# Queries' squared norms of eight heads: from transposes on the matrix engine to block transposes on the vector engine

## The chip, the cores and the metric

The kernel runs on one core of a Trainium2 chip. A core has a matrix engine (PE, with its weight loads shown apart as PEld), a vector engine (DVE), a scalar engine (ACT), a general engine (POOL) and a queue engine (SP) that issues transfers. Each engine works through its own list of instructions in order and waits on semaphores where it needs another's result. The metric is the device time of one execution in microseconds (us).

## The reference

One decoder layer for 1024 prompt tokens (16 learned tokens stand before them) and 8 sample tokens. All head inputs come from one combined projection; two groups of heads follow, four of an mLSTM and eight of a gated delta rule (GDN); a gate, an output projection and a final norm end it. What matters here, for a GDN head (`qg`, `kg` have 128 entries for each token and head):

```
qkv = silu(causal_conv(q|k|v))
qg  = l2norm(qg) * 128 ** -0.5        # x * rsqrt(sum(x * x) + EPS)
kg  = l2norm(kg)
S, og = chunked(gdn_chunk, S, (qg, kg, vg, beta, g))
yg  = head_rms(og) * w_gnorm * silu(z_g)   # h * rsqrt(mean(h * h) + EPS)
```

`og` is linear in `qg`, so a query's norm is only a factor of its output row, and the head norm that follows divides it out again but for its EPS. The kernel therefore leaves the queries unscaled and puts their squared norm into the EPS term of the head norm.

## The kernel before, in words

Everything is kept with features on the 128 partitions and tokens along the free axis. The activations are held as two parts of reduced precision (`xh`, `xl`) and so are the weights (`wh`, `wl`); a projection of one 128-column tile of the weights over all tokens is 3 blocks of tokens by 8 slices of the inner axis by 3 products, 72 matmuls of some 350 columns, written to `pjg` (GDN), `pjz` (gate z of the GDN heads), `pjm` (mLSTM), `pjo` and `pjzm` (gates of the mLSTM heads).

These projections are the filler of PE's list. The generator `filler` walks over the jobs in a fixed order: for each GDN head its k, v and q projections, and after head `h` as many z projections as `ZS[h]` says, then the mLSTM heads, the left z projections, and the gates. All other work (convolutions, the inverse of each head's triangular matrices, the merge, the chains) is written as generators ("threads"), and `Plan.run` records the instructions of all of them in the order in which its own clocks of the engines say that they can go on; when no thread can, the filler gives the next four matmuls. So one order per engine is fixed when the kernel is built. `Plan.note` holds the durations that the planner reckons with; for a vector instruction they go by the size of its output.

The change lies in `gdn_chain(h)`, one head's recurrence over a chunk of 16 tokens and eight chunks of 128. Its inner `prepare(c)` turns k and v of the chunk on PE (`tp<-ident,kq`, `tp<-ident,v`), in the kernel before q as well, and makes k.q (`sk<-kq`). ACT squares the turned q and sums along the row (`jq<-tp`, with an accumulator read after it) into `ss[:, 0, c-1]`. A step then goes: `sk<-S` and `tp<-S` on PE, `R` on DVE, `up<-R` on PE, `wv` on ACT, `up<-wv` on PE, the new state `S` and the output rows `oo` on DVE, whose squares go to `ss[:, 1]`. At the chain's end two small DVE instructions put the two sums into `hst[:, 4 + h]`, the buffers of keys, queries and values go back to their rings (`r_kq`, three buffers; `r_v`, four), and `("C", h)` is marked done. `head_norms` waits for all eight and makes the reciprocal roots `rsg` in one go; `gate(8 + h)` scales the output rows by them. Projections of head `h + 3` need the ring buffer that chain `h` gives back.

Of the kernel before, what the change touches and what calls it, by code (L numbers as in the profile page):

```python
# [12 lines left out]
F32 = mybir.dt.float32  # L13
F32R = mybir.dt.float32r
I32 = mybir.dt.int32
AF = mybir.ActivationFunctionType
ALU = mybir.AluOpType
# [3 lines left out]
P = 128  # L21
D = 1024
KT = D // P
META = 16
SEQ = 1024
NS = 8
TP = META + SEQ
NT = TP + NS
MH, GH = 4, 8
NCH = 1 + SEQ // P  # L30
EPS = 1e-6
BIG = 1e30
MDK = 128.0
# [239 lines left out]
RISE = (4, 6, 3)  # L273
MERGE = 0.5
SAMPLE = 1.5
ZS = (1, 2, 2, 0, 1, 1, 0, 1)


def weight_tiles():
# [12 lines left out]
def chunk(c):  # L292
    return (0, META) if c == 0 else (META + P * (c - 1), P)
# [3 lines left out]
def hymba_kernel(ctx: ExitStack, tc: tile.TileContext, a: dict, o: dict):  # L297
    nc = tc.nc
    plan = Plan()
    dve, act, pool, pe = (  # L300
        Engine(plan, n, e) for n, e in (("dve", nc.vector), ("act", nc.scalar), ("pool", nc.gpsimd), ("pe", nc.tensor)))
# [8 lines left out]
    def bank(tag, name):  # L310
        t = ps.tile([P, 512], F32, tag=tag, name=name, bufs=BANKS[tag])
        plan.take(tag, BANKS[tag], t)
        return t

    def room(tag):
        return plan.room(tag, BANKS[tag])

    def pst(name):
        return bank("s", name)

    def pst2(name):
        return bank("k", name)


    ident = cp.tile([P, P], F32, name="ident")
# [98 lines left out]
    gp = ctx.enter_context(tc.tile_pool(name="gp", bufs=1))  # L424
# [17 lines left out]
    wk = ctx.enter_context(tc.tile_pool(name="wk", bufs=2))  # L442
# [6 lines left out]
    hst = gp.tile([P, GH + MH, 8], F32, name="hst")  # L449
# [7 lines left out]
    def w(tag, shape, name, bufs=2):  # L457
        t, names = wk.tile([P] + shape, F32, tag=tag, name=name, bufs=bufs), wnames.setdefault(tag, [""] * bufs)
        plan.follow(t, names[-bufs])
        names.append(t.tensor.name)  # L460
        return t
# [9 lines left out]
    done = set()  # L471

    def has(*key):
        return lambda: key in done
# [5 lines left out]
        xs.append((r, *r.get([D], f"xt{i}")))  # L480

    warm = w("xss", [2], "warm", NCH + 1)
    nrow = wk.tile([1, D], F32, tag="tmp", name="nrow", bufs=1)
    wgr = wp.tile([P, KT, P], F32, tag="wr", name="wrg")
    wgh_ = wk.tile([P, KT, P], F32R, tag="B", name="whg", bufs=1)
    wrs.append(wgr.tensor.name)
# [139 lines left out]
    def settings():  # L626

        pool.memset(phalf, 0.5)
        yield has("xc", 8)
        dve.tensor_scalar(wgh, wgn, 0.5, None, op0=ALU.mult)  # L630
        dve.tensor_scalar(wmq, wmn, 0.25, None, op0=ALU.mult)
        yield lambda: all(("xc", i) in done for i in range(NCH))
        for e in (ebuf[0], ebuf[1], db, wa, wb):
            pool.memset(e, 0.0)
            yield "pool"
        for e in vas:
            pool.memset(e[:, 256:257], 1.0)

    gr = wk.tile([P, NT], F32, tag="E", name="gr", bufs=1)
    gi, gbig = r_kq.get([2 * TP], "gb")  # L640
# [248 lines left out]
    hd = {}  # L889
# [148 lines left out]
    def gdn_chain(h):  # L1038

        yield lambda: ("M", h) in done and ("P", h, 0) in done  # L1040
        q_ = hd[h]
        (kq, v, ki, vi), gm, kap, em0, eb = hd[h, "P"], q_["gm"], q_["kap"], q_["em0"], ebuf[h % 2]
        pre = {}
        ss = w("ss", [2, 8], f"ss{h}")

        def prepare(c):
            c0, T = chunk(c)
            kc, qc = kq[:, 0, c0 : c0 + T], kq[:, 1, c0 : c0 + T]
            tp, sk, pm = pst(f"tp{h}_{c}"), None, None
            pe.transpose(tp[0:T, 0:P], kc, ident)  # L1050
            pe.transpose(tp[0:T, P : 2 * P], v[:, c0 : c0 + T], ident)
            if c > 0:
                pe.transpose(tp[:, 2 * P : 3 * P], qc, ident)
                sk = pst(f"sk{h}_{c}")
                pe.matmul(sk[:, 0:P], kc, qc, start=True, stop=True)
            kt = w("kt", [P], f"kt{h}_{c}")
            vt = w("vt", [P], f"vt{h}_{c}")
            act.activation(vt[0:T], tp[0:T, P : 2 * P], AF.Copy, scale=kap[0:T, 3, c : c + 1])
            act.activation(kt[0:T], tp[0:T, 0:P], AF.Copy, scale=kap[0:T, 2, c : c + 1])
            if c > 0:  # L1060
                jq = w("jm", [256], f"jq{h}_{c}", bufs=1)[:, 0:P]
                act.activation(jq, tp[:, 2 * P : 3 * P], AF.Square, accum_out=ss[:, 0, c - 1 : c])
                pm = w("pm", [P], f"pm{h}_{c}")
                dve.scalar_tensor_tensor(
                    out=pm, in0=sk[:, 0:P], scalar=kap[:, 1, c : c + 1], in1=gm[:, c, :], op0=ALU.mult, op1=ALU.mult)
            pre[c] = kt, vt, pm, tp, sk

        prepare(0)
        S = None
        yield pre[0][1]  # L1070
        for c in range(NCH):
            c0, T = chunk(c)
            kc, qc = kq[:, 0, c0 : c0 + T], kq[:, 1, c0 : c0 + T]
            kt, vt, pm, tp, sk = pre.pop(c)
            E2 = em0[0:T, 0:T] if c == 0 else eb[:, c - 1, :]
            R = vt
            if c > 0:
                pe.matmul(sk[:, P : 2 * P], kc, S, start=True, stop=True)
                pe.matmul(tp[:, 3 * P : 4 * P], qc, S, start=True, stop=True)
                R = w("R", [P], f"R{h}_{c}")  # L1080
                dve.scalar_tensor_tensor(
                    out=R, in0=sk[:, P : 2 * P], scalar=negc[:, c, h : h + 1], in1=vt, op0=ALU.mult, op1=ALU.add)
                qs = w("qs", [P], f"qs{h}_{c}")
                act.activation(qs, tp[:, 3 * P : 4 * P], AF.Copy, scale=egc[:, c, h : h + 1])
                yield R
            up = pst(f"up{h}_{c}")
            wq = up[:, 2 * P : 3 * P]
            pe.matmul(wq[0:T], E2, R[0:T], start=True, stop=True)
            wv = w("wv", [P], f"wv{h}_{c}")
            act.copy(wv[0:T], wq[0:T])  # L1090
            if c + 1 < NCH:
                prepare(c + 1)
            yield wv
            pe.matmul(up[:, 0:P], kt[0:T], wv[0:T], start=True, stop=True)
            if c > 0:
                pe.matmul(up[:, P : 2 * P], pm, wv, start=True, stop=True)
            Sn = w("S", [P], f"S{h}_{c}", bufs=3)
            if c == 0:
                dve.tensor_copy(Sn, up[:, 0:P])
            else:  # L1100
                dve.scalar_tensor_tensor(
                    out=Sn, in0=S, scalar=egend[:, c, h : h + 1], in1=up[:, 0:P], op0=ALU.mult, op1=ALU.add)
                oo = w("oo", [258], f"oo{h}_{c}", 3)[:, 0:P]
                dve.tensor_tensor(out=oo, in0=qs, in1=up[:, P : 2 * P], op=ALU.add)
                jq = w("jm", [256], f"jo{h}_{c}", bufs=1)[:, 0:P]
                act.activation(jq, oo, AF.Square, accum_out=ss[:, 1, c - 1 : c])
                sp.dma_start(h_d[8 + h, :, c - 1, :], oo)
            S = Sn
            yield S
        yield ss  # L1110
        dve.tensor_scalar(ss[:, 0], ss[:, 0], EPS * MDK, 4 * EPS * EPS * MDK, op0=ALU.mult, op1=ALU.add)
        dve.scalar_tensor_tensor(
            out=hst[:, 4 + h, :], in0=ss[:, 1], scalar=1.0 / P, in1=ss[:, 0], op0=ALU.mult, op1=ALU.add)
        sp.dma_start(o["p_S"][h], S)
        r_gm.free(q_["gi"])
        r_kq.free(ki)
        r_v.free(vi)
        done.add(("C", h))

    def rsqrt_wide(y, x, t):  # L1120

        dve.tensor_scalar(y.bitcast(I32), x.bitcast(I32), -0.5, float(0x5F3759DF), op0=ALU.mult, op1=ALU.add)
        for _ in range(3):
            dve.tensor_tensor(out=t, in0=y, in1=y, op=ALU.mult)
            dve.tensor_tensor(out=t, in0=t, in1=x, op=ALU.mult)
            dve.tensor_scalar(t, t, -0.5, 1.5, op0=ALU.mult, op1=ALU.add)
            dve.tensor_tensor(out=y, in0=y, in1=t, op=ALU.mult)
# [455 lines left out]
    def head_norms():  # L1583

        for heads in ([("C", h) for h in range(GH)], *([("mC", h)] for h in range(MH))):
            yield lambda: all(k in done for k in heads)
            h0 = heads[0][1] if len(heads) == 1 else MH
            n = slice(h0, h0 + len(heads))
            yield hst
            rsqrt_wide(rsg[:, n], hst[:, n], rst[:, 0 : len(heads)])  # L1590
            for i in range(len(heads)):
                done.add(("rs", h0 + i))
# [298 lines left out]
    def filler():  # L1891
        gdn, z = [list(gdn_jobs(h)) for h in range(GH)], [z_job(h) for h in range(GH)]
        jobs = [gate_job]
        for h, n in enumerate(ZS):
            jobs += gdn[h]
# [61 lines left out]
    def chains():  # L1957
        for h in range(GH):
            yield from gdn_chain(h)
        for h in range(MH):  # L1960
            yield from mlstm_chain(h)
# [94 lines left out]
```

## Time and profile before

| | before |
|---|---|
| three runs, median | 1205.81 us (1203.74 to 1205.92) |
| profiled execution, its own time | 1202.72 us |
| its span, from the first to the last instruction | 1200.9 us |
| PE busy | 1184.0 us, 99% |
| DVE, ACT, POOL busy | 852.2, 602.4, 487.9 us |

The 1.8 us between own time and span lie outside the first and last instruction. A busy share is an average: PE's ends are modelled, and matmuls overlap, so the distance from one start to the next says more than the length of one. The chains of the GDN heads fill about 167 to 614 us of the span.

### The profile page before, as it was taken

What the parts mean: (1) busy time and instruction counts of PE and PEld (TensorE: products, weight loads), DVE (VectorE), ACT (ScalarE), POOL (GpSimd) and SP (SyncE); (2) the same over time, 40 slices, a digit from 0 to 9 for tenths busy, and PEclk for the clock granted to TensorE, in tenths of its full rate; (3) what the DMA queues carried; (4) which work ended last, traced back from release to release, by engine and by line L of the source; (5) the groups of instructions that cost most, each with busy time, mean ns of one, the idle gap of its engine ahead of it and who ended that gap; (6) DMA issues with size and microseconds to landing.
All of it is one profiled execution on the core that took longest, in us unless ns stands there. A gap on an engine that the chain in (4) does not pass through costs nothing.

```text
span 1200.9 us, 23024 instructions
## 1 busy us (share of the span) xinstructions
PE 1184.0 (99%) x8314; PEld 1105.9 (92%) x8314; DVE 852.2 (71%) x2069; ACT 602.4 (50%) x1894; POOL 487.9 (41%) x648
## 2 busy tenths in 40 slices
PE   9999999999999999999999999999999999999997
PEld 7999999999999999999999999999999999876885
DVE  6789787587968588864356665546767665887986
ACT  7544455667565666554544453336543433333544
POOL 3105977827685756864012404230011111441432
PEclk9999999999999999999999999999999999999999
DMA  6032212212221221122122443535778878574352
GB/s 242 19 97 86 81 47 83 87 43 72 69 75 43 89 73 55 36 75 61 43 84 70 154 126 119 174 123 172 273 273 286 305 269 297 204 270 132 107 159 87
DMA packets 87084, 154.86 MB, mean 129 GB/s; under 512 B 26793, under 2 KB 48513, under 8 KB 86970
## 3 DMA queue, kind: packets, MB, share of 16 engines
q1 hardware_dynamic: 86776, 153.23, 38.1%
q8 instruction: 65, 1.06, 0.4%
q14 instruction: 49, 0.40, 0.1%
q10 hardware_dynamic: 194, 0.17, 0.0%
HBM read 107.65 MB, written 45.71 MB: 128 GB/s over the span
## 4 chain that ended last, share of the span: by engine, by line
PE 82%; DVE 9%; issue 5%; ACT 1%; POOL 1%; DMA 1%; POOLq 0%; SPq 0%; DVEq 0%; ACTq 0%
PE pjg L56 20%; PE pjm L56 13%; PE pjo L56 7%; PE pjz L56 7%; PE op L56 7%; PE pjzm L56 7%; PE up L56 4%; PE tp L56 3%; PE sk L56 2%; PE mnm L56 2%; DVE left L56 1%; PE mup L56 1%; PE hT L56 1%; DVE owl L56 1%; PE kk L56 1%
## 5 line engine op out<-in xcount | busy, mean ns | idle before, releaser
L56 PE MATMUL pjg<-xht,whg 128*128 128x350 f32 (+6 forms) x624 | 197.6, 324 | 1.0 <-ACT xht L56 1.0
L56 PE MATMUL pjg<-xlt,whg 128*128 128x350 f32 (+6 forms) x624 | 197.1, 323 | 0.0
L56 PE MATMUL pjg<-xht,wlg 128*128 128x350 f32 (+6 forms) x592 | 191.1, 326 | 0.0
L56 POOL TENSOR_TENSOR tmp<-B,E 33x31 f32<-33x31 f32 (+15 forms) x248 | 147.0, 593 | 75.3 <-DMA B<-nd 56.5
L56 POOL TENSOR_TENSOR E<-E,tmp 33x31 f32<-33x31 f32 (+15 forms) x248 | 156.0, 629 | 19.4
L56 PE MATMUL op<-owh,left 128*128 128x512 f32 x448 | 142.0, 396 | 2.1 <-DVE xr L56 1.8
L56 PE MATMUL pjm<-xht,wlm 128*128 128x350 f32 (+2 forms) x384 | 126.4, 329 | 0.0
L56 PE MATMUL pjm<-xht,whm 128*128 128x350 f32 (+2 forms) x384 | 126.4, 329 | 0.0
L56 PE MATMUL pjm<-xlt,whm 128*128 128x350 f32 (+2 forms) x384 | 126.2, 329 | 0.0
L56 PEld LDWEIGHTS pjg<-xht,whg 128*128 128x128 f32 x624 | 116.5, 189 | 1.8 <-issue 1.2
L56 PEld LDWEIGHTS pjg<-xlt,whg 128*128 128x128 f32 x624 | 116.5, 189 | 0.5
L56 PEld LDWEIGHTS pjg<-xht,wlg 128*128 128x128 f32 x592 | 111.0, 189 | 0.4
L56 PEld LDWEIGHTS op<-owh,left 128*128 128x128 f32 x448 | 84.0, 188 | 24.7 <-DVE xr L56 2.6
L56 DVE SCALAR_TENSOR_TENSOR kq<-cr,prm,kq 128x346 f32<-128x346 f32 (+7 forms) x147 | 92.1, 630 | 11.6 <-ACT cr L56 8.3
L56 PE MATMUL op<-owl,left 128*128 128x512 f32 x224 | 88.3, 394 | 0.0
L56 PEld LDWEIGHTS pjm<-xht,wlm 128*128 128x128 f32 x384 | 72.5, 189 | 0.8 <-issue 0.4
L56 PEld LDWEIGHTS pjm<-xlt,whm 128*128 128x128 f32 x384 | 72.4, 188 | 0.6 <-issue 0.4
L56 PEld LDWEIGHTS pjm<-xht,whm 128*128 128x128 f32 x384 | 72.4, 189 | 0.2
L56 POOL TENSOR_TENSOR ebuf<-ebuf,wb 128x1024 f32<-128x1024 f32 x8 | 15.7, 1965 | 122.7 <-DMA ebuf<-mvb_d 122.7
L56 PE MATMUL pjo<-xht,who 128*128 128x344 f32 x192 | 62.3, 324 | 0.6 <-DVE mg L56 0.6
L56 PE MATMUL pjz<-xlt,whz 128*128 128x344 f32 x192 | 62.8, 327 | 0.0
L56 PE MATMUL pjz<-xht,wlz 128*128 128x344 f32 x192 | 62.4, 325 | 0.0
(353 smaller groups left out, 3180.7 us busy)
## 6 DMA issues: line engine op xcount, KB each, us to landing
wrg<-in_wt SPq DMA_DIRECT2D x23, 512.0 KB
left<-c_d SPq DMA_DIRECT2D x40, 256.0 KB
wrm<-in_wt SPq DMA_DIRECT2D x16, 512.0 KB
ht<-h_d SPq DMA_DIRECT2D x16, 512.0 KB
gm<-rows_d SPq DMA_DIRECT2D x8, 576.0 KB
xt<-in_x_p SPq DMA_DIRECT2D x8, 512.0 KB
wrz<-in_wt SPq DMA_DIRECT2D x8, 512.0 KB
h_d<-oo SPq DMA_DIRECT2D x64, 64.0 KB
```

What stands on the lines that cost most here:

```text
L56: r = f(*args, **kw)
```

## The change

The transposes of q leave `prepare`, and with them the square and the accumulator read on ACT. A new thread `query_squares(h)`, started with the chain, takes the head's 1024 tokens of q in four pieces of 256: ACT squares a piece as it lies (features on partitions), DVE turns it in square blocks of 32 by 32, and DVE sums each block row, so that 8 sums for each partition are left (`squares[:, h, 8 * i : 8 * i + 8]`). A partition then holds, for 32 tokens, the sum over only 32 of the 128 features; the other three quarters stand on the other groups of 32 partitions. When all eight chains are done, `query_norms` adds the four groups for all heads in one product on PE with a 0/1 matrix `fold` (128 by 128, into 256 columns, `qsum`), and four DVE instructions add the result to `hst`. `fold` is built in `settings` by three small DVE and three small ACT instructions. The buffers of a head are given back only when its squares are made (`has("Q", h)`). One z projection moves from behind head 4 to behind head 3 (`ZS`). `nrow`, a row used at the start, takes another buffer (`E`), which makes room for the new tiles.

```diff
-ZS = (1, 2, 2, 0, 1, 1, 0, 1)
+ZS = (1, 2, 2, 1, 0, 1, 0, 1)
...
-    nrow = wk.tile([1, D], F32, tag="tmp", name="nrow", bufs=1)
+    nrow = wk.tile([1, D], F32, tag="E", name="nrow", bufs=1)
...
+        f0 = fold[:, 0:32]
+        dve.tensor_tensor(out=f0, in0=ident[:, 0:32], in1=ident[:, 32:64], op=ALU.add)
+        for i in (2, 3):
+            dve.tensor_tensor(out=f0, in0=f0, in1=ident[:, 32 * i : 32 * i + 32], op=ALU.add)
+        for i in (1, 2, 3):
+            act.copy(fold[:, 32 * i : 32 * i + 32], f0)
...
         ss = w("ss", [2, 8], f"ss{h}")
+        plan.add(query_squares(h))
...
             if c > 0:
-                pe.transpose(tp[:, 2 * P : 3 * P], qc, ident)
                 sk = pst(f"sk{h}_{c}")
...
             if c > 0:
-                jq = w("jm", [256], f"jq{h}_{c}", bufs=1)[:, 0:P]
-                act.activation(jq, tp[:, 2 * P : 3 * P], AF.Square, accum_out=ss[:, 0, c - 1 : c])
                 pm = w("pm", [P], f"pm{h}_{c}")
...
-        dve.tensor_scalar(ss[:, 0], ss[:, 0], EPS * MDK, 4 * EPS * EPS * MDK, op0=ALU.mult, op1=ALU.add)
-        dve.scalar_tensor_tensor(
-            out=hst[:, 4 + h, :], in0=ss[:, 1], scalar=1.0 / P, in1=ss[:, 0], op0=ALU.mult, op1=ALU.add)
+        dve.tensor_scalar(hst[:, 4 + h, :], ss[:, 1], 1.0 / P, 4 * EPS * EPS * MDK, op0=ALU.mult, op1=ALU.add)
         sp.dma_start(o["p_S"][h], S)
+        yield has("Q", h)
         r_gm.free(q_["gi"])
...
+    squares = gp.tile([P, GH, 32], F32, name="squares")
+    fold = gp.tile([P, P], F32, name="fold")
+
+    def query_squares(h):
+
+        q = hd[h, "P"][0][:, 1, META:TP]
+        for i in range(4):
+            yield "act"
+            sq, turned = w("sq", [256], f"sq{h}_{i}", bufs=1), w("sqt", [256], f"sqt{h}_{i}", bufs=1)
+            act.activation(sq, q[:, 256 * i : 256 * i + 256], AF.Square)
+            yield sq
+            yield "dve"
+            dve.transpose(turned, sq)
+            dve.tensor_reduce(squares[:, h, 8 * i : 8 * i + 8], turned.rearrange("p (b d) -> p b d", d=32), mybir.AxisListType.X, ALU.add)
+        done.add(("Q", h))
+
+    def query_norms():
+
+        yield squares
+        yield room("k")
+        pt = pst2("qsum")
+        pe.matmul(pt[:, 0 : 32 * GH], fold, squares.rearrange("p h b -> p (h b)"), start=True, stop=True)
+        yield pt
+        for r in range(4):
+            rows = slice(32 * r, 32 * r + 32)
+            part = pt[rows, 0 : 32 * GH].rearrange("p (h c r) -> p h c r", h=GH, r=4)[:, :, :, r]
+            dve.scalar_tensor_tensor(out=hst[rows, MH : MH + GH, :], in0=part, scalar=EPS * MDK, in1=hst[rows, MH : MH + GH, :], op0=ALU.mult, op1=ALU.add)
...
             yield lambda: all(k in done for k in heads)
+            if len(heads) > 1:
+                yield from query_norms()
```

PE's list has 6375 rows before and 6312 after: 64 fewer transposes, one product more. In head 7's chain (names carry head and chunk) the step from `R7_1` to `wv7_1` stood so on PE before:

```order
L56 MATMUL up7_1_8191<-R7_1_8183,ebuf1_102 128x128
L56 MATMUL tp7_2_8195<-ident_65,kq7_6587 128x128
L56 MATMUL tp7_2_8195<-ident_65,v7_6588 128x128
L56 MATMUL tp7_2_8195<-ident_65,kq7_6587 128x128
L56 MATMUL sk7_2_8199<-kq7_6587 128x128
```

and the same step in the changed kernel, with the four projection matmuls that stand behind it:

```order
L56 MATMUL up7_1_8230<-R7_1_8214,ebuf1_102 128x128
L56 MATMUL tp7_2_8234<-ident_65,kq7_6463 128x128
L56 MATMUL tp7_2_8234<-ident_65,v7_6464 128x128
L56 MATMUL sk7_2_8237<-kq7_6463 128x128
L56 MATMUL pjm0_3_2_8224<-xlt_77,whm0_3_7997 128x348
L56 MATMUL pjm0_3_2_8224<-xht_76,wlm0_3_7998 128x348
L56 MATMUL pjm0_3_2_8224<-xht_76,whm0_3_7997 128x348
L56 MATMUL pjm0_3_2_8224<-xlt_77,whm0_3_7997 128x348
L56 MATMUL up7_1_8230<-wv7_1_8232,kt7_1_8183 128x128
```

The second transpose from `kq7` (that of q) is gone; as before, four projection matmuls stand between `sk` and `up<-wv`. On DVE the same chain read before, from `R7_1` to `S7_2`:

```order
L56 SCALAR_TENSOR_TENSOR R7_1_8183<-sk7_1_8152,negc_88,vt7_1_8155 128x128
L56 SCALAR_TENSOR_TENSOR pm7_2_8207<-sk7_2_8199,kap7_6940,gm7_6234 128x128
L56 SCALAR_TENSOR_TENSOR S7_1_8215<-S7_0_8167,egend_90,up7_1_8191 128x128
L56 TENSOR_TENSOR oo7_1_8217<-qs7_1_8185,up7_1_8191 128x128
L56 SCALAR_TENSOR_TENSOR R7_2_8232<-sk7_2_8199,negc_88,vt7_2_8202 128x128
L56 SCALAR_TENSOR_TENSOR pm7_3_8256<-sk7_3_8248,kap7_6940,gm7_6234 128x128
L56 SCALAR_TENSOR_TENSOR S7_2_8266<-S7_1_8215,egend_90,up7_2_8240 128x128
```

and in the changed kernel, from `oo7_1` on:

```order
L56 TENSOR_TENSOR oo7_1_8253<-qs7_1_8216,up7_1_8230 128x128
L56 STREAM_TRANSPOSE sqt7_2_8221<-sq7_2_8220 128x256
L56 TENSOR_REDUCE squares_151<-sqt7_2_8221 128x8
L56 SCALAR_TENSOR_TENSOR R7_2_8275<-sk7_2_8237,negc_88,vt7_2_8240 128x128
L56 SCALAR_TENSOR_TENSOR pm7_3_8296<-sk7_3_8290,kap7_6940,gm7_6395 128x128
L56 STREAM_TRANSPOSE sqt7_3_8267<-sq7_3_8266 128x256
L56 TENSOR_REDUCE squares_151<-sqt7_3_8267 128x8
L56 SCALAR_TENSOR_TENSOR S7_2_8306<-S7_1_8251,egend_90,up7_2_8283 128x128
```

Pairs of a block transpose and a reduction now stand between `oo` and `R` and between `pm` and `S`. Of the 32 such pairs in the list, 16 have an `R` or an `S` as the chain's next instruction behind them, the others a `pm`, or another pair first. The third place is PE's list where the projections of head 3 end. Before, head 4's first projection `pjg4_1` followed at once:

```order
L56 MATMUL pjg3_0_2_3713<-xht_76,whg3_0_3366 128x344
L56 MATMUL pjg3_0_2_3713<-xlt_77,whg3_0_3366 128x344
L56 MATMUL pjg3_0_2_3713<-xht_76,wlg3_0_3367 128x344
L56 MATMUL up2_0_3844<-wv2_0_3846,kt2_0_3827 128x128
L56 MATMUL pjg4_1_0_3879<-xht_76,whg4_1_3680 128x350
```

In the changed kernel the z projection `pjz5` follows, and `pjg4_1` comes behind it:

```order
L56 MATMUL pjg3_0_2_3669<-xlt_77,whg3_0_3323 128x344
L56 MATMUL pjg3_0_2_3669<-xht_76,wlg3_0_3324 128x344
L56 MATMUL pjz5_0_3809<-xht_76,whz5_3615 128x344
L56 MATMUL pjz5_0_3809<-xlt_77,whz5_3615 128x344
L56 MATMUL pjz5_0_3809<-xht_76,wlz5_3616 128x344
```

So 72 matmuls changed places with head 4's 216. The last product of the last GDN chain stands at matmul 3932 of 7141 in PE's list before, and at 3908 of 7078 after.

## Rows read from the trace of the kernel before

**Rows 1.** The page's first part: busy us, share of the span, instructions.

```profile
PE 1184.0 (99%) x8314; PEld 1105.9 (92%) x8314; DVE 852.2 (71%) x2069; ACT 602.4 (50%) x1894; POOL 487.9 (41%) x648
```

**Rows 2.** Stretches: length, busy us of PE, PEld, DVE, ACT, POOL; clock, DMA, GB/s.

```profile
160.00:620.00 460.00, 459.15 (x3758) 442.26 (x3753) 322.94 (x908) 269.85 (x981) 277.21 (x442) 1.00 0.21 63
620.00:1026.00 406.00, 403.03 (x2744) 384.72 (x2743) 254.60 (x637) 175.72 (x534) 82.94 (x63) 1.00 0.57 199
1026.00:1201.00 175.00, 165.30 (x744) 128.03 (x742) 147.19 (x195) 73.83 (x144) 63.37 (x31) 0.99 0.49 164
```

**Rows 3.** PE's waits: total us, times, longest.

```profile
PE op L56 <- DVE xr L56: 1.8, 2, 1.4
...
PE up L56 <- DVE cr L56: 0.4, 1, 0.4
```

**Rows 4.** Timeline of PE, one step of a chain: start, length in us.

```profile
304.08 0.38 PE L56 MATMUL up<-R,ebuf 128*128 128x128 f32 x2
304.30 0.27 PE L56 MATMUL tp<-ident,kq 128*128 128x128 f32 x1
304.41 0.27 PE L56 MATMUL tp<-ident,v 128*128 128x128 f32 x1
304.52 0.27 PE L56 MATMUL tp<-ident,kq 128*128 128x128 f32 x1
304.63 0.39 PE L56 MATMUL sk<-kq 128*128 128x128 f32 x2
```

**Rows 5.** Tile tp: count, ns least/median/most, first and last start.

```profile
L56 PE MATMUL tp<-ident,kq x136: 272/273/329, 167.1 to 610.9; 128*128 128x128 f32 x128, 128*16 128x128 f32 x8
...
L56 ACT ACTIVATE jq<-tp x64: 249/277/323, 170.4 to 611.7; 128x128 f32<-128x128 f32 x64
L56 ACT ACTIVATION_READ_ACCUMULATOR jq<-tp x64: 186/211/257, 170.6 to 611.9; 128x1 f32 x64
```

**Rows 6.** Timeline of PE in an mLSTM chain.

```profile
697.73 0.60 PE L56 MATMUL mnm<-C,mwq 128*128 128x257 f32 x2
698.16 0.60 PE L56 MATMUL mnm<-va,mpm 128*128 128x257 f32 x2
```

**Rows 7.** Groups of DVE: busy us, mean ns; idle us before them, releaser.

```profile
L56 DVE SCALAR_TENSOR_TENSOR pm<-sk,kap,gm 128x128 f32<-128x128 f32 x64 | 22.4, 350 | 50.6 <-PE sk L56 50.1
L56 DVE SCALAR_TENSOR_TENSOR R<-sk,negc,vt 128x128 f32<-128x128 f32 x64 | 22.2, 347 | 25.7 <-PE sk L56 22.0 <-ACT cr L56 1.9 <-ACT mkq L56 0.9
L56 DVE SCALAR_TENSOR_TENSOR S<-S,egend,up 128x128 f32<-128x128 f32 x64 | 22.1, 345 | 21.9 <-PE up L56 14.0 <-issue 4.9 <-ACT whm L56 0.8
L56 DVE STREAM_TRANSPOSE db<-ebuf 32x256 f32<-32x256 f32 x48 | 20.9, 435 | 1.5 <-ACT ebuf L56 0.3
...
L56 DVE TENSOR_TENSOR oo<-qs,up 128x128 f32<-128x128 f32 x64 | 17.9, 280 | 0.0
```

**Rows 8.** Groups of ACT: a square of 256 columns.

```profile
L56 ACT ACTIVATE mjk<-mho 128x256 f32<-128x256 f32 x32 | 13.4, 418 | 1.0
```

**Rows 9.** Timeline of head 7's chain, all engines; idle time in brackets.

```profile
603.04 0.35 DVE L56 SCALAR_TENSOR_TENSOR pm<-sk,kap,gm 128x128 f32<-128x128 f32 x1 [1.20 <-PE sk L56]
...
604.17 0.35 DVE L56 SCALAR_TENSOR_TENSOR S<-S,egend,up 128x128 f32<-128x128 f32 x1 [0.78 <-PE up L56]
...
605.18 0.38 PE L56 MATMUL sk<-S,kq 128*128 128x128 f32 x2
...
605.67 0.35 DVE L56 SCALAR_TENSOR_TENSOR R<-sk,negc,vt 128x128 f32<-128x128 f32 x1 [0.96 <-PE sk L56]
...
606.26 0.38 PE L56 MATMUL up<-R,ebuf 128*128 128x128 f32 x2
```

**Rows 10.** The chain that ended last, in order of time: two z projections.

```profile
117.56 22.83 PE pjz L56 x144
```

**Rows 11.** Tile hT: the transposes that need the head norms.

```profile
L56 PE MATMUL hT<-ident,ht x128: 270/272/329, 817.2 to 1029.3; 128*128 128x128 f32 x128
```

**Rows 12.** The chain that ended last, after the last projection.

```profile
1026.32 4.62 DMA regionxh<-in_wo
```

## The prediction

> **What bounds the kernel now.** I read the page's shares first: PE is busy for 99% of the span, DVE for 71%, ACT for 50% [rows 1]. A share can hide a stage with another limit, so next the stretches. From 160 to 620 us, where the GDN chains run, PE is busy 459.15 of 460 us and DVE 322.94 (70%); from 620 to 1026 PE is busy 403.03 of 406; only in the last stretch does it fall, to 165.30 of 175, and the granted clock is 1.00 until then [rows 2]. The waits agree: the longest of PE in total is 1.8 us, in the output products, and the one in a GDN chain that is worth naming is 0.4 us, at one `up` [rows 3]. So in the stage of the change, and for 400 us behind it, PE's own list is the bound: time taken out of it comes off the end, unless a new wait fills the hole. A ring, DMA or DVE that were late would show as idle time of PE, and almost none is there.
>
> **What is removed from PE.** A transpose lasts 273 ns in the tile's view [rows 5], but matmuls overlap, so its price is the distance between starts. In one step `up`, three transposes and `sk` start at 304.08, 304.30, 304.41, 304.52 and 304.63 us [rows 4]: each transpose takes 0.110 us of PE's list. There are 8 heads by 8 chunks = 64 of them (the 136 in the tile's row are 64 of k, 64 of q and 8 of the small first chunks). 64 x 0.110 = 7.0 us. The removed one stood between two others, so the switches from and to projection matmuls stay.
>
> By the Trainium skill, page "TensorE: Matmul & The Clock Gate", section "Part 4: PE-mode transpose", a transpose costs about 275 ns in a kernel; that is the length in our row, 273 ns, and not the spacing. Were it the price, 64 of them would be worth 17.6 us and the sum would end near 1186 us.
>
> **What is added to PE.** One product of 256 columns, `qsum`, in plain f32. The nearest row is an mLSTM product of 257 columns: two of these start 0.43 us apart, both passes included [rows 6]. So 0.43 us. It stands behind the last chain's end, reads `squares`, whose last pair was made chunks earlier, and nobody needs its result before the first `hT`, at 817.2 us, some 200 us later [rows 11]; its four DVE instructions and the norms behind them lie in that time.
>
> **What moves to ACT and DVE.** ACT loses 64 squares of 0.277 us and 64 accumulator reads of 0.211 us, 31.2 us busy [rows 5], and gets 32 squares of 256 columns; the nearest row with that shape is 418 ns [rows 8], 13.4 us. ACT gets freer, and it was not the bound: I count nothing. DVE gets 32 pairs. The block transpose of 256 columns is there on 32 partitions, 435 ns [rows 7]; the partitions work side by side, so I take the same. The reduction is not in the trace: it reads 256 elements and writes 8. Below it lies `oo`, 128 columns, at 280 ns, above it the block transpose itself, 435 ns [rows 7]; I take 0.40, nearer to the row that reads as much. A pair is then 0.83 us (0.72 to 0.87), 32 of them 27 us, and DVE rises from 70% to about 76% of that stretch.
>
> That alone costs nothing. What counts is whether a pair makes a chain instruction late. DVE stands idle for the chain: 50.6 us ahead of 64 `pm` (0.79 each), 25.7 ahead of `R` (0.40), 21.9 ahead of `S` (0.34) [rows 7]. In the last chains the idle time is larger: 1.20 ahead of `pm`, 0.78 ahead of `S`, 0.96 ahead of `R` [rows 9], so a pair fits or overhangs by 0.05. And PE comes later still: `S` ends at 604.52 and `sk<-S` starts at 605.18, 0.66 later; `R` ends at 606.02 and `up<-R` starts at 606.26, 0.24 later [rows 9]. An overhang must use up this slack before PE waits. Half of the pairs, 16, have an `R` or `S` next behind them. By the mean idle times a pair overhangs an `R` or `S` by 0.83 - 0.37 = 0.46 us; less a slack of 0.24 that leaves 0.22, 16 times: 3.5 us. By the step of head 7 it leaves nothing. Convolutions fill DVE in the first six chains, yet the planner puts a pair where its own clock of DVE sees room. It reckons a reduction by its 8 outputs, though, not by the 256 that it reads, so its room is some 0.3 us too small each time. Between 0 and 3.5 I take 0.6 us, nearer to the rows of a whole step than to the mean.
>
> **The rest.** `ZS` moves one z projection from behind head 4 to behind head 3. It has 72 matmuls; two of them took 22.83 us [rows 10], so 11.4 us of PE work change places with head 4's projections and their DMA for weights, and none is added. Chain 4 gets its data 11.4 us later, against chain 3, which is not affected; and the last GDN chain still ends at matmul 3908 of the list, 24 places sooner with 64 transposes gone, so the chains are stretched over 40 more matmuls of other work, some 6 us, which runs then in place of later. Head 4's projections, which need the buffers of chain 1, come later, and that covers the later release of these buffers by `has("Q", 1)`. I count nothing for it; the bounds are the wait of 0.4 us that the old order has [rows 3], gained or doubled. `fold` costs three DVE instructions of 32 columns, under 0.280 each [rows 7], and three on ACT, once at the start under the projections; without that cover it would be under 1 us. The buffer of `nrow` makes no new wait: its new neighbour is written only after the products that read `nrow`.
>
> Behind the chains PE's list is the same but for places. The last stretch begins when the last projection ends, since the first weights of that stage are loaded into the space of the activations then (1026.32 [rows 12]); so it moves as a whole.
>
> **The sum.** -7.0 + 0.43 + 0.6 = -6.0 us. The profiled execution took 1202.72 us, so its like would take 1196.7. The median of the runs shown, 1205.81, is 3.1 above it; taken from there, 1199.8 us, which I predict.
>
> **The rivals.** *Slower: DVE holds the chains up.* Place: `R` and `S` behind a pair in the first six chains, where convolutions leave the least room. The gain is 6.55 us before stalls; over 32 pairs the mean stall at which nothing is left is 0.20 us, and with 0.30 us (the reduction's unreckoned time, paid in full each time) it is 9.6 us: 1205.81 - 6.55 + 9.6 = 1208.9. For it: the planner's short reckoning, and the slack of 0.24 at `up<-R`. Against: 16 pairs stand ahead of `pm` or no chain step, with 0.79 us idle, and the mean over 16 would have to be 0.41 us. The Trainium skill, page "VectorE: DVE Perf Modes", section "Rules for kernel authors", speaks against this change: it gives 128 x 128 transposes to TensorE where a PSUM result will do, and calls `tensor_reduce` the slowest DVE operation. No row here shows a reduction. Chance of slower this way 0.06, of a loss that leaves about nothing 0.05.
>
> *No change: the chain's latency was the limit and PE's hole is only moved.* A step waits for `R`, `wv` and `S` in turn; if PE comes 0.110 us sooner to `up<-wv` and waits there, 64 steps give the 7.0 us back: 1205.81 + 0.4 = 1206.2, within 0.2%. For it: 0.24 us of slack is little. Against: projections stand in every step and can be drawn forward, as the last chain's end at 3908 shows, and PE's longest wait in these chains is 0.4 us, once [rows 3]. Chance 0.05.
>
> *No change: a later stage takes it back.* From 620 to 1026 us DMA is busy 0.57 at 199 GB/s [rows 2]; were transfers there on a fixed clock, PE would wait for them up to 6 us: 1205.8. Against: PE is busy 99% there and waits for no load. Chance 0.03.
>
> *Much faster: a transpose is worth its whole length,* 0.273 us: 64 x 0.273 = 17.5, so 1205.81 - 17.5 + 1.0 = 1189.3. The starts in rows 4 contradict it. The Trainium skill's 275 ns (above) would say it. Chance 0.02.
>
> **How the numbers follow.** The forecast has the rest, 0.79: PE-bound, stalls of 0 to 3.5 us, which is a change of -6.55 - 0.6 (the old hole closed too) to -3.0, and the median of three runs moves within the 2.2 us between the runs shown. A change under 0.2% (2.4 us) can't be told from none here. Faster: 0.79 + 0.02, and 0.01 for a rival that keeps a part: 0.82. Within: 0.05 + 0.05 + 0.03 = 0.13, less that 0.01: 0.12. Slower: 0.06. The range: down to 1205.81 - 7.15 - 2.2 = 1196.5, and a little below for places that fall well, 1196; up to where the stalls of the bound (3.5) and the spread stand, 1205.81 - 3.05 + 2.2 = 1205.0. Outside it lie the slower rival, half of the no-change rivals and the much faster one, under 2 in 10.
>
> **What would show it.** In the profile after: `tp<-ident,kq` 72 times in place of 136; `qsum` two passes, some 0.4 us; 32 block transposes of 128 partitions at about 435 ns and 32 reductions at 0.3 to 0.43; DVE near 350 us busy in the stretch of the chains, ACT lower by some 18; PE's waits at `up<-R`, `sk<-S` and `up<-wv` together under 3 us; a span near 1195. The prediction is wrong if PE's busy time falls by 7 us and its waits in the chains rise as much, or if the last projection ends sooner and the last stretch is longer.

## The result, and the profile after

| | before | changed |
|---|---|---|
| median | 1204.38 us (1202.53 to 1205.92, 6 runs) | 1196.39 us (1194.85 to 1197.12, 6 runs) |
| profiled execution, own time | 1202.72 us | 1196.62 us |
| its span | 1200.9 us | 1194.8 us |

The ratio is 0.9936 [0.9925, 0.9947]: 7.7 us faster (9.0 to 6.4). The two profiled executions differ by 6.1 us. The forecast was 6.0 us and 1199.8; the time lies inside the range, 0.4 us above its lower end of 1196. The forecast stood on the median of three runs, 1205.81; from the 1204.38 of all six its 6.0 us lead to 1198.4, 2.0 above what was measured. The page of the changed kernel begins (busy us, share, instructions; answers to [rows 1]):

```profile
PE 1179.6 (99%) x8252; PEld 1099.8 (92%) x8252; DVE 880.5 (74%) x2132; ACT 594.3 (50%) x1801; POOL 487.8 (41%) x648
```

PE lost 4.4 us of busy time, DVE got 28.3 more. The stretches, columns as in [rows 2]:

```profile
160.00:620.00 460.00, 459.58 (x3738) 441.62 (x3737) 346.68 (x961) 263.07 (x890) 277.91 (x445) 1.00 0.21 63
620.00:1026.00 406.00, 403.92 (x2734) 383.58 (x2734) 262.57 (x651) 176.91 (x535) 87.03 (x64) 1.00 0.59 203
```

PE is still full in the chains' stretch, and DVE, now 75% busy there, has not taken its place. PE's list of waits says the same (total us, times, longest; its five longest):

```profile
PE op L56 <- DVE xr L56: 1.4, 1, 1.4
PE rise L56 <- DVE ones L56: 1.0, 1, 1.0
PE pjg L56 <- ACT xht L56: 1.0, 1, 1.0
PE mup L56 <- ACT whzm L56: 0.9, 1, 0.9
PE hT L56 <- ACT va L56: 0.8, 1, 0.8
```

No `up<-R`, `sk<-S` or `up<-wv` stands in this list, nor in its rest. The new instructions, in the views of the tiles `tp`, `squares`, `sqt` and `sq` (count, ns least/median/most, first and last start):

```profile
L56 PE MATMUL tp<-ident,kq x72: 270/273/329, 167.4 to 610.8; 128*128 128x128 f32 x64, 128*16 128x128 f32 x8
...
L56 DVE TENSOR_REDUCE squares<-sqt x32: 419/420/422, 201.2 to 591.8; 128x8 f32<-128x256 f32 x32
...
L56 PE MATMUL qsum<-squares,fold x2: 378/378/378, 618.6 to 618.8; 128*128 128x256 f32 x2
...
L56 DVE STREAM_TRANSPOSE sqt<-sq x32: 429/434/445, 200.7 to 591.3; 128x256 f32<-128x256 f32 x32
...
L56 ACT ACTIVATE sq<-kq x32: 399/417/444, 169.2 to 589.1; 128x256 f32<-128x256 f32 x32
```

A pair on DVE is 0.434 + 0.420 = 0.854 us. Where it went is seen in DVE's groups (busy us, mean ns; idle us ahead and its releaser), which answer to [rows 7]:

```profile
L56 DVE SCALAR_TENSOR_TENSOR pm<-sk,kap,gm 128x128 f32<-128x128 f32 x64 | 22.2, 347 | 35.0 <-PE sk L56 34.5
L56 DVE SCALAR_TENSOR_TENSOR R<-sk,negc,vt 128x128 f32<-128x128 f32 x64 | 22.2, 346 | 17.4 <-PE sk L56 14.6 <-PE tp L56 1.3 <-ACT msam L56 0.9
L56 DVE SCALAR_TENSOR_TENSOR S<-S,egend,up 128x128 f32<-128x128 f32 x64 | 22.0, 343 | 23.3 <-PE up L56 20.8 <-ACT mv L56 1.7 <-ACT cr L56 0.3
```

Ahead of `pm` the idle time fell from 50.6 to 35.0 us, ahead of `R` from 25.7 to 17.4, ahead of `S` it stayed: the pairs (27.3 us) fill time in which DVE waited for PE. One new wait did appear, in ACT's list:

```profile
ACT sq L56 <- DVE sqt L56: 8.3, 12, 1.6
```

ACT can't write the next piece of squares before DVE has turned the last one, since `sq` has one buffer. The prediction has no such wait in it. Here it holds nobody up, but it turned out to matter.

### The profile page after: what moved, and what is told of

Its sections match the earlier page's. It is cut to its first block, busy times and chain, and to the rows that moved or that the text cites. A ratio compares the mean times of both kernels' runs of the same rounds, so it can differ in the third digit from the quotient of the medians.

```text
span 1194.8 us, 22870 instructions
## 1 busy us (share of the span) xinstructions
PE 1179.6 (99%) x8252; PEld 1099.8 (92%) x8252; DVE 880.5 (74%) x2132; ACT 594.3 (50%) x1801; POOL 487.8 (41%) x648
## 4 chain that ended last, share of the span: by engine, by line
PE 89%; DVE 6%; DMA 1%; issue 1%; ACT 1%; POOLq 0%; POOL 0%; SPq 0%; DVEq 0%; ACTq 0%
PE pjg L56 22%; PE pjm L56 14%; PE op L56 10%; PE pjz L56 7%; PE pjo L56 7%; PE pjzm L56 7%; PE up L56 4%; PE tp L56 3%; PE sk L56 2%; PE mnm L56 2%; PE mup L56 2%; PE hT L56 1%; PE mtp L56 1%; PE kk L56 1%; PE E L56 1%
## 5 line engine op out<-in xcount | busy, mean ns | idle before, releaser
L56 POOL TENSOR_TENSOR ebuf<-ebuf,skn 128x1024 f32<-128x1024 f32 x8 | 15.9, 1989 | 119.8 <-DMA ebuf<-vb_d 119.8
L56 ACT ACTIVATE jo<-oo 128x128 f32<-128x128 f32 x64 | 19.9, 312 | 86.6 <-DVE oo L56 81.1
L56 PE MATMUL pjz<-xht,whz 128*128 128x344 f32 x192 | 62.6, 326 | 0.0
```

The source lines that it names most:

```text
L56: r = f(*args, **kw)
```

## The experiments

In every table line the ratio is to the kernel before, run on the same chip. The median of the kernel before was 1204.32, 1204.19 and 1204.70 us in the three sets of runs (a, b, c); differences between kernels are taken from the medians of the runs.

| run | median, us | ratio |
|---|---|---|
| a1: changed kernel, `ZS` as before | 1203.85 | 0.9997 [0.9988, 1.0006] |
| a2: kernel before, `ZS` as changed | 1200.43 | 0.9968 [0.9957, 0.9979] |
| a3: changed, 64 transposes back, planner reckons with them | 1211.14 | 1.0057 [1.0037, 1.0076] |
| a4: changed, without the queries' norms | 1195.82 | 0.9929 [0.9917, 0.9940] |
| b1: changed, 64 transposes back, order kept | 1203.24 | 0.9990 [0.9982, 0.9999] |
| b2: a1 with a second buffer for the squares | 1199.05 | 0.9957 [0.9945, 0.9969] |
| b3: changed with a second buffer | 1195.57 | 0.9926 [0.9914, 0.9938] |
| b4: a1, planner prices a reduction by its input | 1205.55 | 1.0008 [1.0000, 1.0017] |
| c1: changed, each DVE pair twice | 1212.85 | 1.0063 [1.0049, 1.0077] |
| c2, c3: kernel before, profiled again | 1204.19, 1206.28 | one run each |

### What the 64 transposes are worth (a3, b1)

The first try puts q's transpose back into `prepare`, with nobody reading it:

```diff
+                pe.transpose(tp[:, 2 * P : 3 * P], qc, ident)
                 sk = pst(f"sk{h}_{c}")
```

> The changed kernel with the 64 transposes of q put back on PE; nobody reads them, the norms come the new way. Theory: each takes 0.11 us of PE's list, so 7.0 us more than the changed kernel, a span near 1202 us and 0.9985 to 1.001 of the kernel before. Rival 1 (a transpose lies partly in holes of the list): 2 to 5 us more. Rival 2 (a transpose costs its whole length of 0.273 us): 17 us more, 1.008 of the kernel before.

It lost 14.7 us, 0.23 for each transpose, which looks like the rival's 0.273. But the planner had reckoned with them and made another order, and the profile of a3 shows a new wait there (timeline of PE: start, length, idle time ahead with its releaser):

```profile
635.77 0.66 PE L56 MATMUL pjm<-xht,whm 128*128 128x350 f32 x1 [3.05 <-ACT mkq L56]
```

with a granted clock of 0.66 in the 5 us from 635. So a3 measures the transposes and an order together, and settles nothing. b1 issues the same instruction past the planner, so that the order on every engine is that of the changed kernel:

```diff
+                nc.tensor.transpose(tp[:, 2 * P : 3 * P], qc, ident)
                 sk = pst(f"sk{h}_{c}")
```

> The changed kernel with the 64 transposes of q put back on PE, unread, and not told to the planner, so that all other instructions stand in the order of the changed kernel. Theory 1 (a transpose takes 0.11 us of PE's list, and what the planner made of it is apart): 6 to 7.5 us more than the changed kernel, a span of 1201 to 1202.5 us, no new wait over 1 us. Theory 2 (the changed kernel gains by fewer waits, not by PE's list): 0 to 3 us more.

1203.24 - 1196.39 = 6.85 us, 0.107 for each; by the spans (1202.1 and 1194.8) 0.114. The page of b1 begins

```profile
PE 1187.1 (99%) x8316; PEld 1107.3 (92%) x8316; DVE 882.3 (73%) x2132; ACT 596.6 (50%) x1801; POOL 485.7 (40%) x648
```

and the list of PE's waits in b1

```profile
PE op L56 <- DVE xr L56: 1.4, 1, 1.4
PE rise L56 <- DVE ones L56: 1.0, 1, 1.0
```

The list goes on as that of the changed kernel does, and only PE's busy time grew, by 7.5 us. The price is the spacing of 0.110 us from [rows 4]; 0.273 would have given 17.5 us and falls. No later stage takes the time back either: the last `hT` starts at 1031.0 us in b1 and at 1023.9 in the changed kernel, 7.1 us sooner.

### What the new way costs (a4)

This kernel leaves out the squares, the pairs, `fold`'s product and the four DVE instructions:

```diff
-        plan.add(query_squares(h))
...
-        yield has("Q", h)
...
-            if len(heads) > 1:
-                yield from query_norms()
```

> The changed kernel without squares, block transposes, reductions, the folding product and its four additions: the queries' norms are left out of the result (the small term of the head norm). It shows what the new way costs. Theory: 0.43 us for the product and 0 to 0.6 us for stalls, so 0.4 to 1.1 us faster than the changed kernel, 0.9925 to 0.993 of the kernel before. Rival (the 32 pairs on DVE make chain steps late): 2 to 4 us faster than the changed kernel, 0.990 to 0.992.

It is 0.6 us below the changed kernel by the medians (0.8 by the ratios, 0.5 by the spans), of which the forecast has 0.43 for the product. By these medians the stalls that 32 pairs made are worth 0.4 us at most; the intervals of the two ratios overlap, and a4 was planned anew too, so this is an estimate. Its stretch from 160 to 620 us also shows what the removed work was on ACT:

```profile
160.00:620.00 460.00, 459.92 (x3743) 442.19 (x3737) 325.99 (x908) 253.69 (x858) 275.44 (x442) 1.00 0.22 64
```

ACT stands at 253.69 without either way, 269.85 with the old one [rows 2], 263.07 with the new one: 16.2 us and 9.4 us of busy time, where lengths summed gave 31.2 and 13.4.

### What the moved z projection is worth (a1, a2)

```diff
-ZS = (1, 2, 2, 1, 0, 1, 0, 1)
+ZS = (1, 2, 2, 0, 1, 1, 0, 1)
```

> The changed kernel with the z projection put back behind head 4. Theory (the gain is the 64 transposes that left PE's list; the z projection only changes places): as the changed kernel, 0.9925 to 0.9945 of the kernel before, a span of 1194 to 1196 us. Rival (the moved z projection gives a part, by covering the later release of keys and queries): 1.5 to 4 us slower than the changed kernel, 0.995 to 0.997 of the kernel before, with a wait of PE of over 1 us between heads 3 and 5.

a2 has the opposite edit, in the kernel before:

```diff
-ZS = (1, 2, 2, 0, 1, 1, 0, 1)
+ZS = (1, 2, 2, 1, 0, 1, 0, 1)
```

> The kernel before with the z projection moved and nothing else. Theory: 0.999 to 1.001 of the kernel before, a span of 1200 to 1202 us. Rival: the move gives a part of the gain by itself, 0.997 to 0.9985, or costs without the rest, over 1.0015.

| medians, us | z as before | z moved |
|---|---|---|
| old norms | 1204.3 | 1200.4 |
| new norms | 1203.9 | 1196.4 |

With z left in its place the new norms gave 0.5 us, no difference that can be told; with z moved they gave 4.0. The move alone gave 3.9; with the new norms it gave 7.5. "I count nothing for it" was wrong by either line, and both effects are larger than the rivals of the two expectations had them. The profile of a1 shows the place. Its timeline of PE (start, length, idle time ahead) goes, where head 4's projections now stand:

```profile
272.92 0.69 PE L56 MATMUL W<-db,N 128*64 128x64 f32 x16 [0.73 <-DVE db L56]
...
276.40 0.32 PE L56 MATMUL pjg<-xlt,whg 128*128 128x350 f32 x1
278.93 0.39 PE L56 MATMUL up<-vt,em 16*16 16x128 f32 x2 [2.21 <-ACT vt L56]
...
282.37 0.49 PE L56 MATMUL pjg<-xht,wlg 128*128 128x350 f32 x1
282.66 0.49 PE L56 MATMUL pjg<-xht,whg 128*128 128x350 f32 x1
```

PE waited 2.21 us for `vt`. What ACT did meanwhile:

```profile
276.90 0.42 ACT L56 ACTIVATE sq<-kq 128x256 f32<-128x256 f32 x1 [2.50 <-DVE sqt L56]
277.34 0.77 ACT L56 ACTIVATE ebuf<-E 64x256 f32<-64x256 f32 x2
278.01 0.48 ACT L56 ACTIVATE cr<-kq 128x346 f32<-128x346 f32 x1
278.52 0.36 ACT L56 ACTIVATE vt<-tp,kap 16x128 f32<-16x128 f32 x1
```

And DVE:

```profile
273.70 2.26 DVE L56 SCALAR_TENSOR_TENSOR kq<-cr,prm,kq 128x346 f32<-128x346 f32 x4
275.88 0.63 DVE L56 SCALAR_TENSOR_TENSOR kq<-cr,kq 128x346 f32<-128x346 f32 x1
276.44 0.43 DVE L56 STREAM_TRANSPOSE sqt<-sq 128x256 f32<-128x256 f32 x1
```

Read from the bottom up: five convolution taps hold DVE for 2.7 us, the block transpose stands behind them; ACT's next square needs the one buffer that this transpose reads and waits 2.50 us; `vt`, which the chain needs, stands behind that square and three more instructions in ACT's list; and PE stands at `up`. Then it costs as much again. The stretches of a1 around it (columns as in [rows 2]):

```profile
275.00:280.00 5.00, 2.79 (x22) 2.21 (x19) 3.18 (x9) 2.93 (x10) 4.29 (x10) 0.99 0.09 38
280.00:285.00 5.00, 5.00 (x19) 4.40 (x18) 2.68 (x7) 0.76 (x3) 4.45 (x8) 0.50 0.00 0
285.00:290.00 5.00, 5.00 (x32) 5.00 (x32) 2.73 (x7) 4.17 (x15) 4.45 (x8) 0.83 0.05 12
```

The granted clock is 0.50, the level of 1.2 GHz, for 5 us and, by the 0.83, for a third of the next 5: some 6.7 us in which PE does half, 3.3 us lost. With the waits of 2.21 and 0.73, and one of 0.46 at `E` between them, that is 6.7 us. The view of the tile `pjg` has the first and last start of one kind of product, in a1 and in the changed kernel:

```profile
L56 PE MATMUL pjg<-xht,whg x624: 277/322/661, 14.9 to 513.9; 128*128 128x350 f32 x56, 128*128 128x346 f32 x32, 128*128 128x348 f32 x28, 128*128 128x344 f32 x16
```

```profile
L56 PE MATMUL pjg<-xht,whg x624: 277/321/431, 15.6 to 508.4; 128*128 128x350 f32 x56, 128*128 128x346 f32 x32, 128*128 128x348 f32 x28, 128*128 128x344 f32 x16
```

The last one starts 5.5 us sooner in the changed kernel, and the last `hT` at 1023.9 in place of 1029.3: what a1's profile loses, it loses ahead of 514 us. Counted from the first one, which came 0.7 us later in the changed kernel's profile, the loss is 6.2 us.

### Is it the buffer, or the planner's price? (b2, b3, b4)

b2 keeps z in the old place and gives every other piece of squares a buffer that is free at that time; b3 has the same edit with z moved:

```diff
-            sq, turned = w("sq", [256], f"sq{h}_{i}", bufs=1), w("sqt", [256], f"sqt{h}_{i}", bufs=1)
+            sq = vas[0][:, 0:256] if i % 2 else w("sq", [256], f"sq{h}_{i}", bufs=1)
+            turned = w("sqt", [256], f"sqt{h}_{i}", bufs=1)
```

> The changed kernel with the z projection put back behind head 4, as in the first run, and the squares of odd pieces in a second buffer (a tile of the mLSTM heads that is idle then). Theory (with the z projection in its old place ACT's next square waits for DVE to turn the last one, the value vt stands behind it and PE waits, and its clock falls): the wait of 2.2 us at up<-vt and the 6.8 us at half clock are gone, 1196 to 1199.5 us, 0.993 to 0.9965 of the kernel before. Rival (the old place itself is bad, through the rings or the chains): as the first run, 0.999 to 1.001.

> The changed kernel with the second buffer for the squares and nothing else. Theory: the waits of ACT for DVE there (8.3 us in 12 times) lie beside PE's work in the changed kernel, so 0.5 us slower to 1 us faster than it, 0.9925 to 0.994 of the kernel before. Rival: they cost PE something, 1 to 3 us faster than the changed kernel.

b4 keeps one buffer and z in the old place, and lets `Plan.note` reckon a reduction by what it reads:

```diff
+            n = max(n, free(ins[0])) if op == "tensor_reduce" else n
```

> The changed kernel with the z projection put back behind head 4 and the planner told that a reduction goes by its input (256 columns) and not by its 8 outputs; one buffer for the squares. Theory (the wait at up<-vt comes of DVE being later than the planner thinks): most of the wait goes, 1197 to 1201 us, 0.994 to 0.997 of the kernel before. Rival (the convolutions in front of the block transpose, not the reduction, make DVE late there): as the first run, 0.998 to 1.001.

b2 is 4.8 us faster than a1. In its profile ACT's waits for the block transpose are

```profile
ACT sq L56 <- DVE sqt L56: 1.1, 2, 0.7
```

in place of 9.1 us in a1, and the last `pjg` starts at 508.6 us, 0.2 from the changed kernel: the loss of 5.5 us ahead of 514 is gone, and with it every wait of PE over 0.15 us from 270 to 285 us. So the chain of waits told above is its cause. b2 was planned anew, though, and in its list no square stands between `wb` and this `vt`, as one does in a1: what a second buffer does with a1's order kept is not shown. b2 is still 2.7 us slower than the changed kernel, and it loses that later, at one place of its own (timelines of ACT and of PE):

```profile
630.65 0.36 ACT L56 ACTIVATE su<-su 128x192 f32<-128x192 f32 x1 [6.31 <-DVE su L56]
...
631.48 0.45 PE L56 MATMUL pjm<-xht,whm 128*128 128x350 f32 x1 [2.16 <-ACT msam L56]
```

with a granted clock of 0.68 from 630 to 635 us. b4 shows that the price was not it, since the wait at `up` is still there:

```profile
PE up L56 <- ACT vt L56: 2.3, 1, 2.3
```

The wait of `sq` is 11.9 us, and the time is that of a1 or worse. That fits the rival, the convolutions ahead of the block transpose, which no run changed by themselves. b3 is 0.8 us below the changed kernel with ACT's wait down from 8.3 to 0.9 us. It is the lowest median of all, but the intervals overlap: a second buffer is insurance there, no gain that can be told.

### How near DVE is to its limit (c1)

```diff
-            dve.transpose(turned, sq)
-            dve.tensor_reduce(squares[:, h, 8 * i : 8 * i + 8], turned.rearrange("p (b d) -> p b d", d=32), mybir.AxisListType.X, ALU.add)
+            for _ in range(2):
+                dve.transpose(turned, sq)
+                dve.tensor_reduce(squares[:, h, 8 * i : 8 * i + 8], turned.rearrange("p (b d) -> p b d", d=32), mybir.AxisListType.X, ALU.add)
```

> The changed kernel with each block transpose and reduction made twice (the same result written twice; the planner knows): 27 us more work for DVE, 82% of the stretch of the chains. Theory (DVE has room, what hurts is the place of single instructions): 0 to 3 us slower than the changed kernel, 0.9936 to 0.996 of the kernel before. Rival (DVE was close to holding the chains up): 4 to 12 us slower, 0.997 to 1.004, with many short waits of PE for R and S.

The first 32 pairs cost some 0.4 us (a4), the second 32 some 16 us, more than either line of the expectation had. The waits in c1's profile, of PE and of ACT:

```profile
PE W L56 <- DVE db L56: 6.2, 2, 4.9
PE up L56 <- DVE R L56: 2.7, 5, 0.8
...
ACT sq L56 <- DVE sqt L56: 30.2, 23, 2.5
```

The slower rival's mechanism exists, then, with DVE at 27 us more. But the larger wait is not at `R`, where the rival put it, but at `W<-db`, where a head's triangular inverse waits for a block transpose; behind the longest of these waits, 4.85 us, the granted clock was 0.50 from 412 to 417 us. The planner knew of the doubled pairs, so part of the 16 us may be its new order.

### Why the medians differ by more than the profiles (c2, c3)

> The kernel before once more, for its profile. Its first profiled execution, 1202.72 us, lies below the median of its other runs, 1204.2 to 1204.4, and the changed kernel's does not. Theory 1 (waits of PE that differ from run to run): a span of 1201 to 1204 us in which PE waits 1 to 3 us more than in the first profile, at places that the changed kernel lacks. Theory 2 (nothing but chance of the same waits): 1200.9 us within 0.5, with the same waits.

> As the run before it, a third profile of the kernel before: 1201 to 1204 us with more waits by theory 1, 1200.4 to 1201.4 us with the same waits by theory 2.

The kernel before was only profiled twice more, without an edit. The same row of PE in c2, in c3 and in the first profile of before:

```profile
690.47 0.69 PE L56 MATMUL mup<-va,mkt 16*128 16x257 f32 x2 [1.86 <-ACT va L56]
```

```profile
690.90 0.70 PE L56 MATMUL mup<-va,mkt 16*128 16x257 f32 x2 [1.19 <-ACT va L56]
```

```profile
688.79 0.69 PE L56 MATMUL mup<-va,mkt 16*128 16x257 f32 x2 [0.23 <-ACT va L56]
```

Ahead of `va` ACT waits for POOL's `mwq`, 2.40 and 1.73 us in c2 and c3 and 0.77 in the first profile. POOL is late because DVE is, and DVE because it waits for a transfer (again c2, c3, the first profile):

```profile
677.37 1.36 DVE L56 TENSOR_TENSOR mgm<-mgm,mt 128x1152 f32<-128x1152 f32 x1 [2.89 <-DMA mgm<-rows_d]
```

```profile
677.82 1.36 DVE L56 TENSOR_TENSOR mgm<-mgm,mt 128x1152 f32<-128x1152 f32 x1 [2.23 <-DMA mgm<-rows_d]
```

```profile
675.75 1.36 DVE L56 TENSOR_TENSOR mgm<-mgm,mt 128x1152 f32<-128x1152 f32 x1 [1.33 <-DMA mgm<-rows_d]
```

SP issued this transfer at 670.02 us in c2 and at 669.97 in the first profile, so it landed later by the 1.6 us that PE waited more. In the changed kernel this row waits for no transfer and this `mup` for nothing. So the first profile of before was a lucky one, with a span 1.5 and 3.6 us below the other two, and the order before was open to a wait that the changed one lacks. By the starts of the same matmuls in both profiles, that is nearly all of the 1.5 us of c2, but only 0.9 of the 3.6 us of c3. Of the rest 0.9 stands in the first 12 us, ahead of all projections, and some 1.7 at 872 us, where ACT waits 3.36 us for the transfer `ht<-h_d` and 1.45 in the first profile. The spreads point the same way: 1202.67 to 1206.98 us over 23 runs of the kernel before, 1202.15 to 1204.37 over 12 of b1, in the same set.

## Why the prediction was right, and where it was not

**PE's list is the bound: right.** 64 transposes were forecast at 7.0 us and measured at 6.85 (b1) by their spacing in [rows 4]. The rivals that a hole on PE gives nothing back, that a later stage takes it back, or that it gives a whole length, all fall with b1. The Trainium skill's 275 ns (page "TensorE: Matmul & The Clock Gate", section "Part 4: PE-mode transpose") agrees with the length, 273 ns, and is not the price in a full list, 107 ns.

**The product and the stalls: right.** 0.43 + 0.6 forecast, 0.5 to 0.8 measured (a4). `qsum` ended at 619 us, and the first `hT`, which needs the norms, came at 809.7.

**The pair on DVE: right in size** (0.854 against 0.83) and in place: PE shows no wait at `R` or `S`. But the chance of 0.06 for the rival that DVE holds the chains up was argued from idle sums of `pm`, `R` and `S` alone. In c1 it decided, and in a1 DVE did hold a chain up, not by its own instruction but through ACT. The rule of the Trainium skill that spoke against the change (page "VectorE: DVE Perf Modes", section "Rules for kernel authors") did not decide: the reduction took 420 ns, less than the block transpose of the same 256 columns (434 ns) and so not the slowest, and DVE had the time where PE had none.

**"I count nothing for it" (`ZS`): the step that failed.** The bounds given, 0.4 us either way, came from the waits of the kernel before. They said nothing of the waits that the new instructions would bring. With z in the old place the planned order puts two squares of a head around a run of convolution taps, and the wait for one buffer costs 5.5 us ahead of 514 us by the profile (7.5 by the medians), which is nearly all of the gain. That this chain of waits is the mechanism is shown by a1 against b2; why the move gives 3.9 us without the new norms is seen only in part: a2's profile has no wait at `pjo` and at `sosum` (0.6 and 0.5 us before), 0.6 us at `op<-xr` (1.8 before) and 0.4 us at `mup<-va`, and one profile can't say how often.

**"ACT lower by some 18": mis-sized.** It fell by 6.8 us in the stretch and 8.1 in all. The lengths of `jq` and of its accumulator's read were added up, though they overlap one another and their neighbours; the whole old way was 16.2 us of ACT's time (a4). ACT was not the bound, so the sum did not suffer.

**The rest of the difference.** Transposes -6.85, new way +0.6 to +0.8; the medians differ by 8.0, which leaves some 1.8 us. The waits of before at `mup` (0.2 to 1.9 us), which the changed order lacks, have that size; that they are all of it is not shown.

**Where it was luck.** The two prices, for the transposes and the new way, were measured in the changed kernel's order. The forecast was for the new norms with the move worth nothing, and no pair of kernels shows that: with z in its old place the norms gave 0.5 us, with z moved 4.0, and neither is the forecast's 6.0. That the whole change came to 8.0, inside the range, took a gain from the move that the sum did not have. Two slips in the margins change nothing: the lower end counts the old hole as 0.6 us where [rows 3] has 0.4, and "near 1186" counts from 1202.72 where the rival's 1189.3 counts from 1205.81.

**Left open.** Why the new norms give 4.0 us from a2, where the two prices add up to some 6.1, is not shown; every kernel but b1 was planned anew. The second place, at 630 to 638 us, where b2 and b4 lose 2.2 us of PE's time behind ACT and a3 some 3, belongs to those orders and was not tried by itself.

## What to carry to other kernels

An instruction taken out of a saturated engine is worth its start-to-start spacing, not its length, as long as the order stays (b1). A new scratch tile with one buffer ties two engines together in both directions: look not only at who reads it, but at what stands behind the next writer in its list, and who waits for that. Where a planner makes the order, try an edit once with the order kept and once planned anew, since the second measures the order as well: b1 lost 6.85 us and a3 14.7 by the same 64 instructions.

## What the runs showed of the hardware

Idle times of PE of 0.73, 0.46 and 2.21 us, shortly one after the other, were followed by some 6.7 us at a granted clock of 0.50, with matmuls 0.29 us apart instead of 0.16 (a1); the fall cost more than the longer wait. A wait of 1.86 us at 690 us in c2 was followed by a clock of 1.00 in the next 8 us. The length of a wait alone did not decide it: ahead of a product `pjm` that waits for `msam`, a wait of 2.16 us in b2 was followed by 0.66 over the next 5 us, with matmuls 0.29 us apart, and one of 2.15 us in b4 by 1.00, with matmuls 0.16 us apart. A block transpose of 256 columns took 434 ns on 128 partitions and 435 on 32, and a reduction of 256 elements to 8 sums took 420 ns, near to the block transpose that reads as much, though it writes only 8 columns. The same transfer, `mgm<-rows_d`, issued at the same time within 0.05 us, landed 1.6 us later in c2 than in the first profile of before.
